# Stick-breaking attention from suffix products and differences of neighbouring values, in place of attention weights

## The chip, the cores and the metric

The kernel runs on one core of one Trainium2 chip. The metric is the device time of one execution in microseconds (us). Before the change three runs gave 1531.31 us as their median (1530.76 to 1535.02).

## The reference, cut to what matters

One layer normalises and modulates a sequence of 2048 rows of 1024 numbers, projects it once to 4232 columns, lets three mixers work on parts of these columns (a gated MLP, an mLSTM, a causal attention of the stick-breaking kind), and projects the gated results back. The change is in the third mixer. It has 6 heads of 64; q and k are normalised; a query block has 128 rows.

```python
z = einsum('bthd,bshd->bhts', q_block, k[:, :kv_len]) * scale
strict = s_idx < t_idx
log_not = where(strict, log_sigmoid(-z), 0)
suffix = cumsum(log_not, reverse=True) - log_not          # over the keys behind s
a = where(strict, exp(log_sigmoid(z) + suffix), 0)
out = einsum('bhts,bshd->bthd', a, v)
```

So a weight is `a_s = sigmoid(z_s)` times the product of `sigmoid(-z)` over the later keys. With `S_s`, the product of `sigmoid(-z)` from key s to the end of the row (1 for masked keys), this is `a_s = S_(s+1) - S_s`. Summed by parts, `sum a_s v_s` is the last value of the row's key range plus `sum S_s (v_(s-1) - v_s)`, with `v_(-1) = 0`.

## The kernel before, in words

The 2048 rows are 16 tiles of 128, in three blocks of 5, 5 and 6 tiles. For each block the modulated rows stay in SBUF, transposed and split in a high and a low part (`hT`); every product with them is three matmuls. The six attention heads are three pairs, p = 0, 1, 2. For every block and pair:

1. `c_proj` projects the pair's q, k and v, one tile at a time: 24 matmuls into one of three PSUM buffers (`pc`). Behind each tile `c_evac` empties the buffer: ScalarE squares q and k (`sq`, L318), VectorE and GpSimd make the scale (`rr`), ScalarE copies v as high part into `Vst` (L323), VectorE writes the low part (L324), and VectorE scales q and k (`qk`, L327). Its second half, one tile later, transposes q and k and writes `Kst` and `Qst`. In the first two blocks the finished pieces go to DRAM for the next block (`k_d`, `v_d`, SyncE's queue).
2. `stick` runs the attention in units: query tile i, head h, up to four key tiles, from the last keys to the first. `front` makes the scores (`z`), two sigmoids on ScalarE (`bb` of -z, L372, and `be` of z, L373), the mask on GpSimd (L375, L377), the suffix product on VectorE (`tensor_tensor_scan`, L380) and the product of both (`be`, L384, units in turn on VectorE and GpSimd). `middle` transposes `be` on TensorE (L395) and splits it in a high and a low part (`aT`: ScalarE L397, VectorE L398). `back` multiplies with `Vst` (L410) and adds the parts (`avs`, `avt`). `fin` sums both halves (`py`), copies (`yc`, L428) and stores. A generator runs front, middle, back and fin one unit apart.

While a pair's units run, the other mixers' projections are woven between them as fillers: `interleave` spreads them by estimated TensorE time. A scheduler then orders the instructions of each engine, by priority and by its own model of time; that order is fixed in the program, and every engine and SyncE's DMA queue works through its list strictly in turn: an instruction that waits holds up all that stand behind it on its engine.

Of the kernel before, what the change touches and what calls it, by code (L numbers as in the profile page):

```python
# [8 lines left out]
F32 = mybir.dt.float32  # L9
F32R = mybir.dt.float32r  # L10
BF16 = mybir.dt.bfloat16
AF = mybir.ActivationFunctionType
ALU = mybir.AluOpType
AX = mybir.AxisListType
PSUM = bass.MemoryType.PSUM
DRAM = bass.MemoryType.DRAM

P = 128
SEQ = 2048
NT = SEQ // P  # L20
# [6 lines left out]
T5 = 6  # L27
OFF = dict(au=0, av=256, az=512, bq=768, bk=1152, bv=1536, bo=1920, bz=2304, bi=2688,
# [4 lines left out]
def hybrid_block_kernel(ctx: ExitStack, tc: tile.TileContext, x, c, norm_g, w_ada, b_ada, w_in,  # L33
                        ga_v_norm, ga_ws, ga_bs, mb_conv_w, mb_conv_b, mb_b_i, mb_b_f, mb_h_norm,
                        sc_q_norm, sc_k_norm, w_out, out):
    nc = tc.nc
# [4 lines left out]
    dram = ctx.enter_context(tc.tile_pool(name="scratch", bufs=1, space=DRAM))  # L41

# [10 lines left out]
    v_d = [dram.tile([P, NT, 2, P], F32, name=f"v_d{p}") for p in range(3)]  # L53

# [1 line left out]
    ident = const.tile([P, P], F32, name="ident")  # L56
# [18 lines left out]
    gates = const.tile([P, 2, NT, 4], F32, name="gates")  # L75
# [69 lines left out]
    def mod_x(i, c0, c1, eng=None):  # L145
        """normalised and modulated, in place"""
        xc = x_cols(i, c0, c1)
        nc.vector.scalar_tensor_tensor(xc, xc, xtiles[i][1], hscale[:, c0:c1], ALU.mult, ALU.mult)
        (eng or nc.gpsimd).tensor_tensor(xc, xc, hshift[:, c0:c1], ALU.add)
# [22 lines left out]
    def weights(src, segs, kps=range(KT // 2), staged=None):  # L172
        """hi and lo parts of the given columns, one tile per 128 rows"""
        W = sum(w for _, w in segs)
        tiles = []
        for kp in kps:
            st = staged[kp] if staged else load_w(src, segs, kp)
            for a in range(2):
                wt = wr_p.tile([P, 2, WMAX], F32R, tag="wr", name=f"wr{ntag[0]}_{kp}_{a}")
                nc.scalar.copy(wt[:, 0, :W], st[:, a, :W])  # L180
                (nc.vector if a == 0 else nc.gpsimd).tensor_tensor(  # L181
                    wt[:, 1, :W], st[:, a, :W], wt[:, 0, :W].bitcast(F32), ALU.subtract)
                tiles.append(wt)
        ntag[0] += 1
        return tiles
# [12 lines left out]
    brow = [stk.tile([P, 512], F32, tag="bb", bufs=4, name=f"brow{n}") for n in range(4)]  # L198
    for n in (2, 0, 3, 1):
        nc.gpsimd.memset(brow[n], 0.0)  # L200
    g_bc = [stk.tile([P, 512], F32, tag="be", bufs=3, name=f"g_bc{n}") for n in range(2)]
# [67 lines left out]
    def hT_half(i, j, hh):  # L269
        """half of the rows of tile j of hT, hi and lo parts"""  # L270
        cols = slice(j * P, (j + 1) * P)
        ks = slice(hh * 4, hh * 4 + 4)
        pt = (pat.tile([P, 4, P], F32, tag="at", name=f"pt{i}_{hh}") if i < BLOCKS[0] else
              pproj.tile([P, 512], F32, tag="proj", name=f"pt{i}_{hh}").rearrange("p (k t) -> p k t", k=4))
        for k in range(4):
            kk = hh * 4 + k
            nc.tensor.transpose(pt[:, k, :], x_cols(i, kk * P, (kk + 1) * P), ident)
        nc.scalar.copy(hT[:, 0, ks, cols], pt)
        nc.vector.tensor_tensor(hT[:, 1, ks, cols], pt, hT[:, 0, ks, cols].bitcast(F32), ALU.subtract)  # L279

    def proj_tc(ps, wt, j, W, ks=range(KT)):
        """psum[t, cols] of t tile j of the block"""
        cols = slice(j * P, (j + 1) * P)
        for k in ks:
            nc.tensor.matmul(ps, lhsT=hT[:, 0, k, cols], rhs=wt[k][:, 0, :W], start=k == 0, stop=False)  # L285
            nc.tensor.matmul(ps, lhsT=hT[:, 0, k, cols], rhs=wt[k][:, 1, :W], start=False, stop=False)  # L286
            nc.tensor.matmul(ps, lhsT=hT[:, 1, k, cols], rhs=wt[k][:, 0, :W], start=False, stop=k == KT - 1)  # L287
            yield 3 * W / 2.4

# [22 lines left out]
    def c_evac(b, t0, p, j, ps):  # L312
        i = t0 + j
        if p == 0:
# [8 lines left out]
        nc.scalar.copy(Vst[:, i, :, 0:64], ps[:, 256:384].rearrange("p (h d) -> p h d", h=2))  # L323
        nc.vector.tensor_tensor(Vst[:, i, :, 64:128], ps[:, 256:384].rearrange("p (h d) -> p h d", h=2),  # L324
                                Vst[:, i, :, 0:64].bitcast(F32), ALU.subtract)
# [6 lines left out]
        for a in range(4):  # L332
# [8 lines left out]
                                       ALU.mult, ALU.subtract)  # L341
        if b < len(BLOCKS) - 1:
            nc.sync.dma_start(k_d[p][:, :, i * P:(i + 1) * P], ks.bitcast(F32))
            nc.sync.dma_start(v_d[p][:, i], Vst[:, i].bitcast(F32))

    def stick(p, t0, nb):
# [12 lines left out]
        st_count = []  # L359

        def front(u):
# [7 lines left out]
            bb = stk.tile([P, 513], F32, tag="bb", bufs=4, name=f"bb{nm}")  # L369
            be = stk.tile([P, 512], F32, tag="be", bufs=3, name=f"be{nm}")  # L370
            nc.gpsimd.memset(bb[:, w:w + 1], 1.0)  # L371
            nc.scalar.activation(bb[:, :w], z[:, :w], AF.Sigmoid, scale=-1.0)  # L372
            nc.scalar.activation(be[:, :w], z[:, :w], AF.Sigmoid)  # L373
            if s1 == i + 1:
                nc.gpsimd.affine_select(out=bb[:, w - P:w], in_=bb[:, w - P:w], pattern=[[-1, P]],  # L375
                                        compare_op=ALU.is_gt, fill=1.0, base=0, channel_multiplier=1)
                nc.gpsimd.affine_select(out=be[:, w - P:w], in_=be[:, w - P:w], pattern=[[-1, P]],  # L377
                                        compare_op=ALU.is_gt, fill=0.0, base=0, channel_multiplier=1)
            rev = bb[:, 0:w + 1][:, ::-1]
            nc.vector.tensor_tensor_scan(rev, rev, rev, carry.get((i, h), 1.0), ALU.mult, ALU.bypass)  # L380
            carry[i, h] = bb[:, 0:1]
            eng = nc.gpsimd if len(st_count) % 2 else nc.vector
            st_count.append(0)
            eng.tensor_tensor(be[:, :w], be[:, :w], bb[:, 1:w + 1], ALU.mult)  # L384
            st[u] = [be, None]
            return 2 * w / 2.4

        def middle(u):
            i, j, h, s0, s1 = u
            nm = f"{p}_{i}_{h}_{s0}"  # L390
            be = st[u][0]
            nb_ = s1 - s0
            at = pat.tile([P, 4, P], F32, tag="at", name=f"at{nm}")
            for s in range(nb_):
                nc.tensor.transpose(at[:, s, :], be[:, s * P:(s + 1) * P], ident)  # L395
# [24 lines left out]
        def fin(u):  # L420
# [7 lines left out]
            nc.scalar.copy(yc, py[:, 0:P])  # L428
# [224 lines left out]
    def first_chunk():  # L653
        """chunk 0 of the mLSTM ahead of the output phase: its gated output and the state after it"""
# [227 lines left out]
    def mlstm(i):  # L882
        """numerator and denominator of chunk i, state after it"""
# [32 lines left out]
    def mixed(i):  # L916
        """the gated outputs of the three mixers, [t, c]"""
# [43 lines left out]
    def chunk_ahead(i):  # L961
        """chunk i from its scores to the turned outputs"""
        yield from mlstm(i)
        mixed(i)
        yield
        yield from turned(i)
# [66 lines left out]
```

## Time and profile before

| | |
|---|---|
| median of three runs | 1531.31 us |
| span of the profiled execution | 1527.0 us |
| outside the span, by the median | 4.3 us |
| TensorE busy (matmul) | 1413.2 us, 93% |
| VectorE busy | 1123.3 us, 74% |
| GpSimd busy | 757.2 us, 50% |
| ScalarE busy | 749.6 us, 49% |
| mean granted TensorE clock | 0.978 of full |

The profile gives the profiled execution's time as its span, 1527.0 us. The attention runs from about 75 us to 1266 us; behind it comes the output phase, which the change leaves alone. Busy time of TensorE counts each matmul with the tail in which its results drain, and matmuls overlap there, so stretches with 100% are those in which no gap is longer than such a tail.

### The profile page before, as it was taken

What the parts mean: (1) busy time and instruction counts of PE and PEld (TensorE: products, weight loads), DVE (VectorE), ACT (ScalarE), POOL (GpSimd) and SP (SyncE); (2) the same over time, 40 slices, a digit from 0 to 9 for tenths busy, and PEclk for the clock granted to TensorE, in tenths of its full rate; (3) what the DMA queues carried; (4) which work ended last, traced back from release to release, by engine and by line L of the source; (5) the groups of instructions that cost most, each with busy time, mean ns of one, the idle gap of its engine ahead of it and who ended that gap; (6) DMA issues with size and microseconds to landing.
All of it is one profiled execution on the core that took longest, in us unless ns stands there. A gap on an engine that the chain in (4) does not pass through costs nothing.

```text
span 1527.0 us, 25375 instructions
## 1 busy us (share of the span) xinstructions
PE 1413.2 (93%) x8468; PEld 1307.1 (86%) x8468; DVE 1123.3 (74%) x1866; ACT 749.6 (49%) x1832; POOL 757.2 (50%) x1228
## 2 busy tenths in 40 slices
PE   5899999889889999988898899999998978999998
PEld 3789999889878999977898699989898956888887
DVE  6787555775997677699699986879968797544444
ACT  2365444454655455557366755656545565211210
POOL 4364544664445544666344554645535246534442
PEclk8899999999999999999999999999999999999999
DMA  9433423334435422523322124112230154546551
GB/s 325 130 92 100 121 80 87 95 109 122 133 93 140 136 69 74 141 53 111 103 63 74 41 63 124 46 48 76 78 89 18 62 189 120 196 128 190 149 158 67
DMA packets 170595, 163.89 MB, mean 107 GB/s; under 512 B 23610, under 2 KB 146904, under 8 KB 170464
## 3 DMA queue, kind: packets, MB, share of 16 engines
q1 hardware_dynamic: 170240, 162.24, 36.1%
q8 instruction: 67, 1.10, 0.3%
q14 instruction: 64, 0.52, 0.1%
q0 software_dynamic: 224, 0.02, 0.0%
HBM read 124.58 MB, written 37.64 MB: 106 GB/s over the span
## 4 chain that ended last, share of the span: by engine, by line
PE 53%; DVE 25%; issue 7%; DMA 6%; POOL 5%; ACT 4%; SPq 0%; DVEq 0%; POOLq 0%; ACTq 0%
DVE bb L380 9%; PE po L946 4%; PE po L948 4%; PE po L947 4%; PE av L410 3%; PE pc L287 3%; DMA st<-in_w_in_dram 3%; PE pc L285 3%; PE pc L286 3%; PE at L395 3%; DVE acc L467 2%; DVE aT L398 2%; PE pg L286 2%; DVE be L384 2%; PE pg L285 2%
## 5 line engine op out<-in xcount | busy, mean ns | idle before, releaser
L380 DVE TENSOR_TENSOR_SCAN bb<-bb,bb 128x513 f32<-128x513 f32 x144 | 198.9, 1382 | 18.4 <-ACT bb L372 18.0
L384 POOL TENSOR_TENSOR be<-be,bb 128x512 f32<-128x512 f32 (+3 forms) x120 | 135.3, 1127 | 125.2 <-DVE bb L380 65.5
L181 POOL TENSOR_TENSOR wr<-st,wr 128x384 fp32r<-128x384 f32 (+1 forms) x132 | 158.4, 1204 | 61.8 <-ACT wr L180 60.0
L180 ACT CAST wr<-st 128x384 fp32r<-128x384 f32 (+1 forms) x264 | 127.3, 522 | 113.0 <-DMA st<-in_w_in_dram 103.2
L410 PE MATMUL av<-aT,Vst 128*128 128x256 f32 x816 | 148.1, 298 | 30.4 <-DVE aT L398 20.8
L410 PEld LDWEIGHTS av<-aT,Vst 128*128 128x128 f32 x816 | 120.6, 192 | 47.5 <-DVE aT L398 30.5
L398 DVE TENSOR_TENSOR aT<-at,aT 128x512 fp32r<-128x512 f32 (+3 forms) x240 | 142.0, 596 | 24.0 <-ACT aT L397 23.6
L372 ACT ACTIVATE bb<-z 128x512 f32<-128x512 f32 (+3 forms) x240 | 131.1, 547 | 53.4 <-PE z L368 47.4
L397 ACT CAST aT<-at 128x512 fp32r<-128x512 f32 (+3 forms) x240 | 126.8, 529 | 51.7 <-PE at L395 50.4
L395 PE MATMUL at<-ident,be 128*128 128x128 f32 x816 | 133.3, 278 | 16.6 <-DVE Qst L340 7.3
L285 PE MATMUL pc<-wr,hT 128*128 128x384 f32 (+1 forms) x384 | 136.0, 356 | 7.2 <-DVE hT L279 6.2
L287 PE MATMUL pc<-wr,hT 128*128 128x384 f32 (+1 forms) x384 | 136.8, 356 | 2.6 <-DVE hT L279 2.6
L181 DVE TENSOR_TENSOR wr<-st,wr 128x384 fp32r<-128x384 f32 (+1 forms) x132 | 103.9, 787 | 47.8 <-ACT wr L180 47.5
L286 PE MATMUL pc<-wr,hT 128*128 128x384 f32 (+1 forms) x384 | 134.7, 351 | 0.0
L373 ACT ACTIVATE be<-z 128x512 f32<-128x512 f32 (+3 forms) x240 | 132.6, 552 | 0.0
L395 PEld LDWEIGHTS at<-ident,be 128*128 128x128 f32 x816 | 98.4, 142 | 28.2 <-DVE aT L398 11.1
L380 DVE TENSOR_TENSOR_SCAN bb<-bb 128x129 f32<-128x129 f32 (+3 forms) x96 | 95.7, 997 | 17.4 <-POOL bb L375 14.5
L946 PE MATMUL po<-wo,yT 128*128 128x512 f32 x256 | 104.8, 409 | 0.3 <-ACT yT L935 0.3
L947 PE MATMUL po<-wo,yT 128*128 128x512 f32 x256 | 102.3, 399 | 0.7 <-POOL wo L853 0.7
L948 PE MATMUL po<-wo,yT 128*128 128x512 f32 x256 | 101.4, 399 | 0.0
L371 POOL MEMSET bb<- 128x1 f32 x240 | 23.4, 98 | 150.6 <-DVE bb L380 98.8
L367 PE MATMUL z<-Kst,Qst 128*128 128x512 f32 (+3 forms) x240 | 93.7, 392 | 3.8 <-ACT be L373 3.7
(272 smaller groups left out, 4098.7 us busy)
## 6 DMA issues: line engine op xcount, KB each, us to landing
st<-in_w_in_dram SPq DMA_DIRECT2D x180, 128.0 KB, 2.4
st<-in_w_in_dram SPq DMA_DIRECT2D x48, 384.0 KB, 3.3
st<-in_w_in_dram SPq DMA_DIRECT2D x48, 192.0 KB, 2.6
wad<-in_w_ada_dram SPq DMA_DIRECT2D x8, 1024.0 KB, 7.3
xo<-in_x_dram SPq DMA_DIRECT2D x16, 512.0 KB, 3.6
out_dram<-o SPq DMA_DIRECT2D x31, 256.0 KB, 2.8
xt<-in_x_dram SPq DMA_DIRECT2D x15, 512.0 KB, 4.4
qk<-qkT_d SPq DMA_DIRECT2D x15, 384.0 KB, 7.5
```

The source lines that it names most:

```text
L181: (nc.vector if a == 0 else nc.gpsimd).tensor_tensor(wt[:, 1, :W], st[:, a, :W], wt[:, 0, :W].bitcast(F32), ALU.subtract)
L285: nc.tensor.matmul(ps, lhsT=hT[:, 0, k, cols], rhs=wt[k][:, 0, :W], start=k == 0, stop=False)
L286: nc.tensor.matmul(ps, lhsT=hT[:, 0, k, cols], rhs=wt[k][:, 1, :W], start=False, stop=False)
L287: nc.tensor.matmul(ps, lhsT=hT[:, 1, k, cols], rhs=wt[k][:, 0, :W], start=False, stop=k == KT - 1)
L380: nc.vector.tensor_tensor_scan(rev, rev, rev, carry.get((i, h), 1.0), ALU.mult, ALU.bypass)
L384: eng.tensor_tensor(be[:, :w], be[:, :w], bb[:, 1:w + 1], ALU.mult)
L395: nc.tensor.transpose(at[:, s, :], be[:, s * P:(s + 1) * P], ident)
L398: nc.vector.tensor_tensor(aT[:, :nb_, 1, :], at[:, :nb_, :], aT[:, :nb_, 0, :].bitcast(F32), ALU.subtract)
L410: nc.tensor.matmul(flat(av), lhsT=Vst[:, s0 + s, h, :], rhs=flat(aT[:, s]), start=(s0 + s == i), stop=(s0 + s == 0))
L946: nc.tensor.matmul(po, lhsT=yT[:, 0, k, :], rhs=wo[k][:, 0, cs], start=k == 0, stop=False)
L947: nc.tensor.matmul(po, lhsT=yT[:, 0, k, :], rhs=wo[k][:, 1, cs], start=False, stop=False)
L948: nc.tensor.matmul(po, lhsT=yT[:, 1, k, :], rhs=wo[k][:, 0, cs], start=False, stop=k == KT - 1)
```

## The change

Only the suffix product `bb` is left in a unit: the second sigmoid (L373), its mask (L377), the memset of a 513th column (L371) and the product (L384) are gone, and `bb` itself is transposed. The values in `Vst` become differences of neighbouring rows. For that `c_evac` copies v to SBUF (`vt`, ScalarE); a DMA moves rows 0 to 126 of `vt` to rows 1 to 127 of another tile (`dv`); row 0 comes from a small DRAM table of last rows (`vl_d`), which each tile writes; GpSimd subtracts; ScalarE and GpSimd write the high and low part. At the end of a query tile `yc` adds the last value, which a DMA has spread over 128 rows (`vlast`), on VectorE. `bb` has six buffers where `bb` and `be` had four and three.

```diff
+    vl_d = dram.tile([3 * NT, P], F32, name="vl_d")
...
-        nc.scalar.copy(Vst[:, i, :, 0:64], ps[:, 256:384].rearrange("p (h d) -> p h d", h=2))
-        nc.vector.tensor_tensor(Vst[:, i, :, 64:128], ps[:, 256:384].rearrange("p (h d) -> p h d", h=2),
-                                Vst[:, i, :, 0:64].bitcast(F32), ALU.subtract)
+        vt = tmp.tile([P, P], F32, tag="vt", name=f"vt{p}_{i}")
+        nc.scalar.copy(vt, ps[:, 256:384])
+        nc.sync.dma_start(vl_d[p * NT + i:p * NT + i + 1, :], vt[P - 1:P, :])
+        dv = tmp.tile([P, P], F32, tag="dv", name=f"dv{p}_{i}")
+        nc.sync.dma_start(dv[1:P, :], vt[0:P - 1, :])
+        if i == 0:
+            nc.gpsimd.memset(dv[0:1, :], 0.0)
+        else:
+            nc.sync.dma_start(dv[0:1, :], vl_d[p * NT + i - 1:p * NT + i, :])
...
+        nc.gpsimd.tensor_tensor(dv, dv, vt, ALU.subtract)
+        dv2 = dv.rearrange("p (h d) -> p h d", h=2)
+        nc.scalar.copy(Vst[:, i, :, 0:64], dv2)
+        nc.gpsimd.tensor_tensor(Vst[:, i, :, 64:128], dv2, Vst[:, i, :, 0:64].bitcast(F32), ALU.subtract)
...
-            bb = stk.tile([P, 513], F32, tag="bb", bufs=4, name=f"bb{nm}")
-            be = stk.tile([P, 512], F32, tag="be", bufs=3, name=f"be{nm}")
-            nc.gpsimd.memset(bb[:, w:w + 1], 1.0)
+            bb = stk.tile([P, 512], F32, tag="bb", bufs=BB, name=f"bb{nm}")
             nc.scalar.activation(bb[:, :w], z[:, :w], AF.Sigmoid, scale=-1.0)
-            nc.scalar.activation(be[:, :w], z[:, :w], AF.Sigmoid)
...
-                nc.gpsimd.affine_select(out=be[:, w - P:w], in_=be[:, w - P:w], pattern=[[-1, P]],
-                                        compare_op=ALU.is_gt, fill=0.0, base=0, channel_multiplier=1)
-            rev = bb[:, 0:w + 1][:, ::-1]
+                if h == 0:
+                    vlast[i] = stk.tile([P, P], F32, tag="vlast", name=f"vlast{p}_{i}")
+                    nc.sync.dma_start(vlast[i], vl_d[p * NT + i:p * NT + i + 1, :].broadcast_to([P, P]))
+            rev = bb[:, 0:w][:, ::-1]
             nc.vector.tensor_tensor_scan(rev, rev, rev, carry.get((i, h), 1.0), ALU.mult, ALU.bypass)
             carry[i, h] = bb[:, 0:1]
-            eng = nc.gpsimd if len(st_count) % 2 else nc.vector
-            st_count.append(0)
-            eng.tensor_tensor(be[:, :w], be[:, :w], bb[:, 1:w + 1], ALU.mult)
...
-            nc.scalar.copy(yc, py[:, 0:P])
+            nc.vector.tensor_tensor(yc, py[:, 0:P], vlast.pop(i), ALU.add)
```

The second half of the difference (the GpSimd and ScalarE lines) stands in the part of `c_evac` that runs one tile later, but the scheduler puts it earlier. On ScalarE, in the second block's first pair (tiles 5 to 9), the order before was this; `sq` is the square of a tile's q and k, `pc` its PSUM buffer:

```order
L318 ACTIVATE sq_5_4193<-pc_5_4153 128x256
L323 CAST Vst<-pc_5_4153 128x2x64
L318 ACTIVATE sq_6_4229<-pc_6_4203 128x256
L323 CAST Vst<-pc_6_4203 128x2x64
L336 ACTIVATE Kst<-pq_5_4239,prm 128x2x128
L337 ACTIVATE Qst<-pq_5_4239,prm 128x256
L318 ACTIVATE sq_7_4276<-pc_7_4250 128x256
L323 CAST Vst<-pc_7_4250 128x2x64
```

The same place on ScalarE now:

```order
L320 ACTIVATE sq_5_4155<-pc_5_4115 128x256
L326 COPY vt_5_4161<-pc_5_4115 128x128
L353 CAST Vst<-dv_5_4164 128x2x64
L320 ACTIVATE sq_6_4195<-pc_6_4169 128x256
L326 COPY vt_6_4201<-pc_6_4169 128x128
L344 ACTIVATE Kst<-pq_5_4209,prm 128x2x128
L345 ACTIVATE Qst<-pq_5_4209,prm 128x256
L353 CAST Vst<-dv_6_4204 128x2x64
L320 ACTIVATE sq_7_4249<-pc_7_4223 128x256
L326 COPY vt_7_4255<-pc_7_4223 128x128
```

The write of a tile's differences now stands ahead of the square of the next tile, and it can run only when the shifted rows have arrived and GpSimd has subtracted.

At the end of the same stage ScalarE's list now holds this (`bb` are sigmoids of the first attention units, `wr` weights of the next filler):

```order
L383 ACTIVATE bb_5_0_4_4402<-z_5_0_4_4399 128x256
L353 CAST Vst<-dv_8_4312 128x2x64
L320 ACTIVATE sq_9_4357<-pc_9_4331 128x256
L182 CAST wr_3_0_4436<-st_3_4434 128x384
L182 CAST wr_3_1_4439<-st_3_4434 128x384
L326 COPY vt_9_4363<-pc_9_4331 128x128
L383 ACTIVATE bb_5_0_0_4452<-z_5_0_0_4449 128x512
L344 ACTIVATE Kst<-pq_8_4371,prm 128x2x128
L345 ACTIVATE Qst<-pq_8_4371,prm 128x256
L383 ACTIVATE bb_5_1_4_4473<-z_5_1_4_4470 128x256
L353 CAST Vst<-dv_9_4366 128x2x64
L383 ACTIVATE bb_5_1_0_4523<-z_5_1_0_4520 128x512
```

Weights of the next filler and the first units' sigmoids stand behind the differences of tiles 8 and 9. On SyncE's DMA queue there are four transfers more per tile:

```order
L327 DMA vl_d<-vt_5_4161 1x128
L329 DMA dv_5_4164<-vt_5_4161 127x128
L333 DMA dv_6_4204<-vl_d 1x128
L389 DMA vlast_5_4407<-vl_d 128x128
L357 DMA v_d_71<-Vst 128x256
L327 DMA vl_d<-vt_6_4201 1x128
L329 DMA dv_6_4204<-vt_6_4201 127x128
```

The store of tile 5's differences (`v_d`) stands ahead of the shift of tile 6.

## Rows read from the trace of the kernel before

**Rows 1.** The page's head and its part 1: busy us, share, instructions.

```profile
span 1527.0 us, 25375 instructions
PE 1413.2 (93%) x8468; PEld 1307.1 (86%) x8468; DVE 1123.3 (74%) x1866; ACT 749.6 (49%) x1832; POOL 757.2 (50%) x1228
```

**Rows 2.** Windows where VectorE is fullest: length; busy of each engine; clock; DMA.

```profile
375.00:500.00 125.00, 112.56 (x710) 103.99 (x709) 109.01 (x173) 68.95 (x170) 65.31 (x110) 0.99 0.43 123
650.00:700.00 50.00, 42.96 (x259) 39.55 (x258) 46.47 (x76) 28.38 (x75) 31.45 (x53) 0.97 0.24 66
770.00:900.00 130.00, 117.31 (x701) 108.27 (x701) 120.77 (x184) 87.59 (x188) 60.57 (x112) 0.97 0.20 57
1050.00:1100.00 50.00, 47.30 (x291) 45.06 (x291) 47.44 (x78) 32.40 (x82) 27.16 (x49) 0.97 0.20 51
1225.00:1266.00 41.00, 30.64 (x193) 24.42 (x192) 37.46 (x47) 24.37 (x52) 14.82 (x28) 0.96 0.41 148
sum 396.00, PE 350.78 PEld 321.30 DVE 361.15 ACT 241.69 POOL 199.31; mean PE 70.16 PEld 64.26 DVE 72.23 ACT 48.34 POOL 39.86
```

**Rows 3.** The same five windows, line L384 (the removed product) alone: their sum.

```profile
sum 396.00, DVE 33.66 POOL 63.11; mean DVE 6.73 POOL 12.62
```

**Rows 4.** Four other windows (75-300, 500-650, 900-1050, 1100-1150), all instructions: their sum.

```profile
sum 575.00, PE 563.79 PEld 547.41 DVE 408.27 ACT 310.48 POOL 295.26; mean PE 140.95 PEld 136.85 DVE 102.07 ACT 77.62 POOL 73.82
```

**Rows 5.** Waits of TensorE: line, waited for; total us, times, longest us.

```profile
PE av L410 <- DVE aT L398: 20.8, 22, 2.6
PE av L410 <- DVE avt L416: 9.5, 11, 1.8
PE at L395 <- DVE aT L398: 7.1, 12, 1.2
```

**Rows 6.** Groups: line, engine, operation, shapes, count; busy us, mean ns; idle before.

```profile
L384 POOL TENSOR_TENSOR be<-be,bb 128x512 f32<-128x512 f32 (+3 forms) x120 | 135.3, 1127 | 125.2 <-DVE bb L380 65.5
L384 DVE TENSOR_TENSOR be<-be,bb 128x512 f32<-128x512 f32 (+3 forms) x120 | 81.3, 677 | 1.9 <-POOL be L377 0.2
L373 ACT ACTIVATE be<-z 128x512 f32<-128x512 f32 (+3 forms) x240 | 132.6, 552 | 0.0
L377 POOL TENSOR_SCALAR_AFFINE_SELECT be<-be 128x128 f32<-128x128 f32 x96 | 40.6, 423 | 20.6 <-ACT be L373 18.1 <-DMA gate_d<-gg 1.1 <-PE pb L455 0.5
L324 DVE TENSOR_TENSOR Vst<-pc,Vst 128x128 fp32r<-128x128 f32 x48 | 13.3, 281 | 2.1 <-ACT Vst L323 2.1
L416 DVE TENSOR_TENSOR avt<-av,avs 128x128 f32<-128x128 f32 x96 | 26.6, 277 | 25.3 <-ACT avs L414 25.1
L533 POOL TENSOR_TENSOR gu<-tb 128x128 f32<-128x128 f32 x32 | 19.8, 618 | 24.4 <-DVE tb L532 23.3 <-PE pa L287 0.8
```

**Rows 7.** Line L380, VectorE: count, duration ns smallest/median/largest.

```profile
L380 DVE TENSOR_TENSOR_SCAN bb<-bb,bb x144: 1268/1278/3400, 114.7 to 1257.9; 128x513 f32<-128x513 f32 x144
```

**Rows 8.** ScalarE in time, 504 to 510 us: start, us, instruction [idle before <-releaser].

```profile
504.77 0.39 ACT L318 ACTIVATE sq<-pc 128x256 f32<-128x256 f32 x1 [2.54 <-PE pc L287]
505.05 0.26 ACT L323 CAST Vst<-pc 128x128 fp32r<-128x128 f32 x1
...
509.42 0.39 ACT L318 ACTIVATE sq<-pc 128x256 f32<-128x256 f32 x1 [1.10 <-PE pc L287]
```

**Rows 9.** Transfers yc to y_d: issue ns on SyncE; KB and us to landing.

```profile
L429 SPq DMA_DIRECT2D y_d<-yc x48: 319/339/1277, 112.3 to 1266.1; - x48
y_d<-yc SPq DMA_DIRECT2D x48, 64.0 KB, 1.7
```

**Rows 10.** DMA, 509.5 to 511 us: one store of k, 256 pieces of 512 bytes.

```profile
DMA packets 272, 0.13 MB, mean 87 GB/s; under 512 B 16, under 2 KB 272, under 8 KB 272
q1 hardware_dynamic: 272, 0.13, 30.8%
```

**Rows 11.** DMA, 1.7 to 2.2 us: one load of 8 rows of 512 bytes.

```profile
DMA packets 16, 0.00 MB, mean 8 GB/s; under 512 B 8, under 2 KB 16, under 8 KB 16
```

More of the change, by code (lines that the diff above doesn't have):

```diff
@@ L27 @@
 T5 = 6
+BB = 6
 OFF = dict(au=0, av=256, az=512, bq=768, bk=1152, bv=1536, bo=1920, bz=2304, bi=2688,
@@ L197, in hybrid_block_kernel @@
     crow = tmp.tile([8, P], F32, tag="t512", bufs=T5, name="crow")
-    brow = [stk.tile([P, 512], F32, tag="bb", bufs=4, name=f"brow{n}") for n in range(4)]
+    brow = [stk.tile([P, 512], F32, tag="bb", bufs=BB, name=f"brow{n}") for n in range(4)]
     for n in (2, 0, 3, 1):
         nc.gpsimd.memset(brow[n], 0.0)
-    g_bc = [stk.tile([P, 512], F32, tag="be", bufs=3, name=f"g_bc{n}") for n in range(2)]
+    g_bc = [stk.tile([P, 512], F32, tag="bb", bufs=BB, name=f"g_bc{n}") for n in range(2)]
     def ada_load(half):
@@ L358, in stick @@
         st = {}
-        st_count = []
+        vlast = {}
         def front(u):
@@ L376, in front @@
                                         compare_op=ALU.is_gt, fill=1.0, base=0, channel_multiplier=1)
-                nc.gpsimd.affine_select(out=be[:, w - P:w], in_=be[:, w - P:w], pattern=[[-1, P]],
-                                        compare_op=ALU.is_gt, fill=0.0, base=0, channel_multiplier=1)
-            rev = bb[:, 0:w + 1][:, ::-1]
+                if h == 0:
+                    vlast[i] = stk.tile([P, P], F32, tag="vlast", name=f"vlast{p}_{i}")
+                    nc.sync.dma_start(vlast[i], vl_d[p * NT + i:p * NT + i + 1, :].broadcast_to([P, P]))
+            rev = bb[:, 0:w][:, ::-1]
             nc.vector.tensor_tensor_scan(rev, rev, rev, carry.get((i, h), 1.0), ALU.mult, ALU.bypass)
             carry[i, h] = bb[:, 0:1]
-            eng = nc.gpsimd if len(st_count) % 2 else nc.vector
-            st_count.append(0)
-            eng.tensor_tensor(be[:, :w], be[:, :w], bb[:, 1:w + 1], ALU.mult)
-            st[u] = [be, None]
+            st[u] = [bb, None]
             return 2 * w / 2.4
@@ L390, in middle @@
             nm = f"{p}_{i}_{h}_{s0}"
-            be = st[u][0]
+            bb = st[u][0]
             nb_ = s1 - s0
@@ L394, in middle @@
             for s in range(nb_):
-                nc.tensor.transpose(at[:, s, :], be[:, s * P:(s + 1) * P], ident)
+                nc.tensor.transpose(at[:, s, :], bb[:, s * P:(s + 1) * P], ident)
             aT = stk.tile([P, 4, 2, P], F32R, tag="aT", bufs=3, name=f"aT{nm}")
```

## The prediction

> **What bounds the kernel now.** I read the busy shares first, then windows by stage, then who TensorE waits for, and last the stretch in which v is written. TensorE is the fullest engine, 93% of a span of 1527.0 us [rows 1], and the change gives it neither more nor fewer matmuls. So the change can only move TensorE's idle time. Its place shows in the windows: in five stretches of the attention, together 396 us, VectorE is busy 361.15 us (91%) and TensorE 350.78, so idle 45.2 us [rows 2]; in four others, 575 us, VectorE is busy 408.27 (71%) and TensorE idle only 11.2 us [rows 4]. TensorE is late where VectorE is full. The waits agree: the three largest of its attention lines end with VectorE, on the split of the transposed weights and on the sum of the two output parts, 20.8 + 9.5 + 7.1 = 37.4 us [rows 5]. [...]
>
> The reader is also to see the start of each attention stage. While a pair's q, k and v are projected, ScalarE waits for TensorE, does the square (0.39 us) and the copy of v (0.26 us), and waits again; one tile follows the other after 509.42 - 504.77 = 4.65 us [rows 8]. Nothing is full there, but everything passes through ScalarE in turn.
>
> **The change part by part.** *What goes.* ScalarE loses the second sigmoid, 240 of 552 ns, 132.6 us [rows 6]. It is not the bound (49%, [rows 1]), so I count nothing for it beyond a shorter way from score to scan. GpSimd loses its share of the product, 135.3 us, and the second mask, 40.6 us [rows 6]; it is not the bound either. VectorE loses 120 products of 677 ns, 81.3 us [rows 6], of which 33.66 us lie in the five full stretches [rows 3]. There it is the late engine, so this part counts: 33.7 us. The rest, 47.6 us, lies mostly where TensorE has hardly any idle time to give back; I count 4 us.
>
> *What eases.* The scan takes 1278 ns in the median and 3400 at the longest for the same shape [rows 7]; GpSimd reads the same memory at those times, and its work falls by 135.3 + 40.6 us and grows by the 59 us below. I take 6 us in the full stretches, between nothing and a sixth of the 45.2 us. So the gain is 33.7 + 4 + 6 = 44 us. Its bounds: nothing, if the fixed order of the instructions keeps TensorE waiting as it does; and 45.2 + 10 = 55 us, all idle time of the five stretches with the clock that it costs.
>
> *What stays even.* VectorE loses the low part of v, 48 of 281 ns [rows 6], and gets the sum into yc, the same number of the same shape from PSUM, nearest to the 277 ns of avt [rows 6]: nothing either way. ScalarE writes v twice instead of once and yc no more: even. `vlast` is asked for as a query tile begins and needed at its end, some units later; I count nothing, and where it came late VectorE's whole list would stand behind it.
>
> *What is added, and waits.* GpSimd gets two 128x128 subtractions per tile, 96 of 618 ns by the nearest row [rows 6], 59 us on a half-empty engine: nothing by itself. But they and ScalarE's write stand in a chain. From the copy of v: SyncE issues the row store and the shift (2 x 0.34 us [rows 9]), the shift lands, GpSimd subtracts (0.62), ScalarE writes the high part (0.26), and only behind it, in ScalarE's list as the change orders it, come the next tile's square (0.39) and copy (0.26). That is 2.21 us plus the landing. If the sum is under the 4.65 us between tiles, the wait costs nothing; if it is over, each tile puts ScalarE further behind, and with it the weights of the next filler, the first sigmoids and the emptying of PSUM buffers, all queued behind the write.
>
> The landing has two bounds. Low: 1.7 us, the median of a transfer of the same 64 KB in the same 512-byte pieces [rows 9]; the chain is 3.9 us, hidden. High: the pieces go one after another. One store of 256 such pieces kept 30.8% of 16 engines busy for 1.5 us, 7.4 us for 272 packets, 27 ns each [rows 10]. The 64 KB of [rows 9] are 128 pieces, 8 for each of 16 engines; 127 on one engine are 119 more in a row, 3.2 us more: landing 4.9 us, chain 7.1 us, 2.5 us too long per tile. Which is nearer? The store of 128 rows closes with 16 small packets [rows 10], the load of 8 rows with 8 [rows 11]: the number of engines follows the rows, with equal shares. 127 is prime, so equal shares leave one engine. I take the high bound, 4.9 us.
>
> [...]
>
> What does it cost? A stage has five or six tiles, so four or five follow-ups of 2.5 us, 10 to 12.5 us by which ScalarE would be late at the end where the chain is whole (the second block's first pair). In other stages the scheduler set two copies ahead of one write, or the tiles come slower, and part of it goes. TensorE can run on for as long as the three `pc` buffers and the two score buffers last, about one to two tiles, 4.65 to 9.3 us. So the loss of a stage lies between nothing and 8 us; I take 4 us, the middle, for nine stages: 36 us.
>
> The sum: 1527.0 - 44 + 36 = 1519 us of span; with the 4.3 us by which the median of the runs stands over this span, 1523 us.
>
> **The rivals.** *A. The shift is hidden.* It lands in about the 1.7 us of its like, or TensorE's lead covers the chain. For it: nothing in the trace waits long for a 64 KB transfer between tiles, and ScalarE has idle time of 1.1 to 2.5 us before each square [rows 8]. Against it: 127 rows have no equal shares. It gives the whole gain: 1527 - 44 + 4 = 1487 us, at best 1527 - 55 + 4 = 1476.
>
> *B. The shift becomes the bound of every stage start: slower.* One mechanism: the rows pass one DMA engine, ScalarE stands at the write of the differences, and TensorE uses up its buffers and stops. It decides once the chain passes 4.65 us by more than the buffers cover, that is, over some 2 us per tile. At 8 us for each of nine stages the loss is 72 us: 1527 - 44 + 72 + 4 = 1559 us; with half of the gain lost too, 1581. For it: the list of ScalarE, and the one engine. Against it: in six of nine stages the writes are grouped behind later squares.
>
> *C. The relief doesn't come.* The full stretches are bound by the order in which the units interleave, not by VectorE's load. Then only a small loss or nothing: 1527 to 1540 us. For it: the idle times are short (the longest wait is 2.6 us [rows 5]). Against it: their release by VectorE nearly everywhere.
>
> **How the numbers follow.** Forecast (both effects, near 1523, with 1505 to 1540 as its own range) 0.42; A 0.26; B 0.27; C 0.05. The range reaches into A and B, from 1478 to 1570 us, and leaves out about 0.08 below and 0.10 above. A measurement of this kernel can tell 0.3%, 4.6 us, from no change. Faster by more: all of A, and over half of the forecast's own case (0.23), 0.49. Within: a quarter of that case and part of C, 0.13. Slower by more: B, a fifth of the forecast's case, and part of C, 0.38.
>
> **What would show it.** In the five stretches VectorE's share should fall from 91% to about 82% and TensorE's waits for aT and avt from 37.4 us to under 20. The shift's transfers should land 4.9 us after issue; a landing near 2 us makes A right. ScalarE should wait at the write of `Vst`, and GpSimd at its subtraction, for the DMA, some microseconds per tile; the squares of successive tiles should lie 7 us apart instead of 4.65 where the chain is whole. TensorE's new idle time should lie in the ten microseconds behind each projection of q, k and v. I am wrong in the size if that idle time is under 15 us or over 60 us in total, and in the mechanism if VectorE's relief leaves its waits as they were.

## The result, and the profile after

The changed kernel takes 1569.27 us (median of four runs, 1566.2 to 1571.08), the kernel before 1533.16 us (four runs beside it, 1530.76 to 1535.09). The ratio is 1.0238, with a 95% interval of 1.0216 to 1.026: slower by 36 us, where 1523 us and a gain were forecast. Rival B came, at 1569 instead of its 1559 us. The head of the page after answers to [rows 1]:

```profile
span 1564.5 us, 24609 instructions
PE 1427.1 (91%) x8468; PEld 1316.1 (84%) x8468; DVE 1015.6 (65%) x1746; ACT 645.5 (41%) x1592; POOL 606.4 (39%) x871
```

Three engines lost 104 to 151 us of work each, and TensorE's count of matmuls is the same. Of the 37.5 us by which the span is longer, 23.6 are new idle time of TensorE (113.8 us before, 137.4 now), and 13.9 are matmuls that took longer. The stages have moved, so the windows of [rows 2] no longer hold the same work. Two stretches do, from the last square of one stage to the first of the next, behind the second block's and the third block's first pair. The first two lines are of the kernel before, the others of the changed one (length; busy us of TensorE, its weight loads, VectorE, ScalarE, GpSimd; clock; DMA):

```profile
384.23:501.53 117.30, 104.86 (x663) 96.42 (x663) 102.58 (x161) 64.42 (x160) 61.28 (x104) 0.99 0.45 126
770.05:924.22 154.17, 141.48 (x857) 131.49 (x856) 138.96 (x211) 102.15 (x219) 74.88 (x132) 0.98 0.21 60
412.05:524.04 111.99, 103.49 (x646) 94.89 (x647) 91.19 (x153) 55.07 (x135) 41.94 (x63) 0.98 0.46 130
818.12:962.90 144.78, 138.56 (x849) 130.60 (x849) 123.81 (x198) 83.70 (x178) 45.09 (x65) 0.98 0.26 76
```

VectorE is down from 87 to 81% in the first and from 90 to 86% in the other, and TensorE's idle time in them from 12.4 to 8.5 us and from 12.7 to 6.2. The relief shows there, so the new idle time lies elsewhere. TensorE's waits in the whole kernel, those of [rows 5] first (total us, times, longest):

```profile
PE av L418 <- DVE aT L406: 10.4, 11, 4.0
PE av L418 <- DVE avt L424: 8.4, 12, 1.2
PE at L403 <- DVE aT L406: 2.1, 4, 0.9
...
PE z L380 <- ACT bb L383: 15.4, 7, 3.2
PE pq L341 <- DVE qk L335: 15.0, 9, 2.9
```

The 37.4 us on aT and avt are 20.9: the relief came. In their place stand waits for ScalarE's sigmoids of the attention units and for the scaled q and k of the projection. The waits of the three engines behind the shift:

```profile
ACT Vst L353 <- POOL dv L351: 193.5, 45, 7.5
POOL dv L351 <- DMA dv<-vt: 117.0, 39, 5.2
DVE qk L335 <- POOL rr L324: 44.4, 32, 4.5
```

ScalarE stands 193.5 us at the write of the differences, in 45 of 48 tiles. ScalarE in time, in the stage of the second block's first pair (compare [rows 8]):

```profile
388.63 0.30 ACT L353 CAST Vst<-dv 128x128 fp32r<-128x128 f32 x1 [6.22 <-POOL dv L351]
388.83 0.38 ACT L320 ACTIVATE sq<-pc 128x256 f32<-128x256 f32 x1
389.11 0.26 ACT L326 COPY vt<-pc 128x128 f32<-128x128 f32 x1
389.25 0.49 ACT L344 ACTIVATE Kst<-pq,prm 128x256 fp32r<-128x256 f32 x1
389.62 0.48 ACT L345 ACTIVATE Qst<-pq,prm 128x256 fp32r<-128x256 f32 x1
396.20 0.30 ACT L353 CAST Vst<-dv 128x128 fp32r<-128x128 f32 x1 [6.09 <-POOL dv L351]
396.40 0.38 ACT L320 ACTIVATE sq<-pc 128x256 f32<-128x256 f32 x1
```

The square no longer waits for TensorE but follows the write at once, 396.40 - 388.83 = 7.57 us after the one before; 4.65 us it was. The chain between, on SyncE's queue and GpSimd:

```profile
389.50 0.34 SPq L357 DMA_DIRECT2D v_d<-Vst  x1
389.93 0.24 SPq L327 DMA_DIRECT2D vl_d<-vt  x1
390.22 0.66 SPq L329 DMA_DIRECT2D dv<-vt  x1
```

```profile
388.13 0.46 POOL L351 TENSOR_TENSOR dv<-dv,vt 128x128 f32<-128x128 f32 x1 [3.73 <-DMA dv<-vt]
389.00 0.46 POOL L354 TENSOR_TENSOR Vst<-dv,Vst 128x128 fp32r<-128x128 f32 x1 [0.41 <-ACT Vst L353]
389.76 0.19 POOL L323 TENSOR_SCALAR rr<-rr 128x4 f32<-128x4 f32 x1 [0.29 <-DVE rr L322]
390.03 1.01 POOL L324 TENSOR_TENSOR rr<-rr,neghalf 128x4 f32<-128x4 f32 x1
395.70 0.46 POOL L351 TENSOR_TENSOR dv<-dv,vt 128x128 f32<-128x128 f32 x1 [4.66 <-DMA dv<-vt]
```

From the shift's issue at 390.22 to the subtraction at 395.70 pass 5.48 us; over the 48 tiles the median is 5.80 (worked out from the start times of the two lines). A stretch of 1.8 us with almost nothing but one shift in it, that of a later tile, shows why (GB/s in 40 equal slices; packets; share of 16 engines):

```profile
GB/s 0 0 0 23 23 0 0 23 23 23 23 23 23 23 23 23 23 11 23 23 23 23 23 23 23 23 23 23 23 11 23 23 23 23 23 23 23 23 23 11
DMA packets 74, 0.03 MB, mean 19 GB/s; under 512 B 7, under 2 KB 74, under 8 KB 74
q1 hardware_dynamic: 74, 0.03, 6.7%
```

From the eighth slice on there are two packets in a slice of 45 ns at most, a steady 23 GB/s; over the stretch 6.7% of 16 engines are busy, which is 1.07 engines. Ahead of it, packets of this shift begin 1.3 us after its issue (802.24 us), another transfer of 192 KB passes between them, and the row of them ends at 807.3: 5.1 us, where 4.9 were predicted. GpSimd's subtraction comes only at 808.26.

### The profile page after: what moved, and what is told of

Its sections match the earlier page's. It is cut to its first block, busy times and chain, and to the rows that moved or that the text cites. A ratio compares the mean times of both kernels' runs of the same rounds, so it can differ in the third digit from the quotient of the medians.

```text
span 1564.5 us, 24609 instructions
## 1 busy us (share of the span) xinstructions
PE 1427.1 (91%) x8468; PEld 1316.1 (84%) x8468; DVE 1015.6 (65%) x1746; ACT 645.5 (41%) x1592; POOL 606.4 (39%) x871
## 5 line engine op out<-in xcount | busy, mean ns | idle before, releaser
L391 DVE TENSOR_TENSOR_SCAN bb<-bb,bb 128x512 f32<-128x512 f32 x144 | 193.0, 1341 | 9.4 <-ACT bb L383 8.5
L183 POOL TENSOR_TENSOR wr<-st,wr 128x384 fp32r<-128x384 f32 (+1 forms) x132 | 154.6, 1175 | 104.9 <-ACT wr L182 97.5
L403 PE MATMUL at<-ident,bb 128*128 128x128 f32 x816 | 133.2, 276 | 17.1 <-DVE Qst L348 10.6
L403 PEld LDWEIGHTS at<-ident,bb 128*128 128x128 f32 x816 | 98.6, 141 | 27.5 <-issue 10.2
L380 PE MATMUL z<-Kst,Qst 128*128 128x512 f32 (+3 forms) x240 | 95.1, 399 | 19.5 <-ACT bb L383 15.4
L461 PE MATMUL pb<-hT,wr 128*128 128x320 f32 (+1 forms) x288 | 95.7, 333 | 10.1 <-ACT wr L182 4.3
L385 POOL TENSOR_SCALAR_AFFINE_SELECT bb<-bb 128x128 f32<-128x128 f32 x96 | 43.5, 455 | 152.9 <-ACT bb L383 131.6
L391 DVE TENSOR_TENSOR_SCAN bb<-bb 128x128 f32<-128x128 f32 (+3 forms) x96 | 83.6, 874 | 26.0 <-POOL bb L385 25.7
L463 PE MATMUL pb<-hT,wr 128*128 128x320 f32 (+1 forms) x288 | 94.5, 330 | 3.6 <-POOL wr L183 2.8
```

Of the source, the lines that this page charges most:

```text
L183: (nc.vector if a == 0 else nc.gpsimd).tensor_tensor(wt[:, 1, :W], st[:, a, :W], wt[:, 0, :W].bitcast(F32), ALU.subtract)
L403: nc.tensor.transpose(at[:, s, :], bb[:, s * P:(s + 1) * P], ident)
```

## The experiments

Theory 1: the 127 rows pass one DMA engine, and what stands behind their landing in the lists of ScalarE and GpSimd holds TensorE up. The main rival: the loss is that of more transfers, of another order, or of a relief that doesn't come. "Stretch" below is the time from the first to the last square (L320), summed over the nine stages, and "to subtraction" the median from the shift's issue to GpSimd's subtraction; both are worked out from start times in the trace. Ratios are to the kernel before, on the same chip.

| kernel | us | ratio, 95% interval | to subtraction, us | stretch, us |
|---|---|---|---|---|
| before | 1530 to 1533 | 1 | | 197.2 |
| after | 1569.27 | 1.0238 (1.0216 to 1.026) | 5.80 | 241.1 |
| relief alone | 1480.24 | 0.965 (0.9634 to 0.9667) | | 189.5 |
| chain alone | 1612.63 | 1.052 (1.0505 to 1.0536) | 5.35 | 248.2 |
| cut 113 + 14 | 1550.05 | 1.0111 (1.0086 to 1.0135) | 5.53 | 225.9 |
| cut 122 + 5 | 1504.88 | 0.9831 (0.981 to 0.9853) | 4.02 | 196.7 |
| cut 126 + 1 | 1499.46 | 0.9778 (0.9764 to 0.9793) | 3.61 | 191.1 |
| cut 112 + 15, first | 1489.80 | 0.9736 (0.9696 to 0.9775) | 3.31 | 190.1 |
| high part by GpSimd | 1543.44 | 1.0073 (1.0044 to 1.0102) | 5.83 | 208.1 |
| tied to the next tile | 1520.90 | 0.9933 (0.991 to 0.9956) | 7.35 | 188.5 |
| tied, cut 112 + 15 | 1486.74 | 0.971 (0.9686 to 0.9735) | 7.56 | 191.9 |

**The shift in two, 126 + 1 and 113 + 14.** The two cuts have the same number of transfers, one more than the change; the second has 113 and 14 in place of the two numbers of rows.

```diff
-        nc.sync.dma_start(dv[1:P, :], vt[0:P - 1, :])
+        nc.sync.dma_start(dv[1:P - 1, :], vt[0:P - 2, :])
+        nc.sync.dma_start(dv[P - 1:P, :], vt[P - 2:P - 1, :])
```

> The shift of 127 rows is issued as two transfers, one of 126 rows and one of the last row; the data is the same. Theory 1 (the 127 rows pass one DMA engine; the write of the differences stands in ScalarE's list behind them at every stage start): 126 has the divisor 14, so nine rows on each of 14 engines; from the issue to GpSimd's subtraction 2 to 3.5 us instead of 5.8, squares of neighbouring tiles 4.6 to 5.5 us apart instead of 7.6, ScalarE's wait at the write of Vst from 193.5 us to under 60, and the time 1485 to 1505 us. Theory 2 (the loss is that of the two more transfers per tile in SyncE's queue and of a third engine in the chain, whatever the shift takes): there is one transfer more, so 1565 to 1580 us.

> The same edit with another cut: 113 rows and 14 rows, the same number of transfers as in the cut of 126 and 1. 113 is prime. Theory 1: 113 rows still pass one engine, 14 x 27 ns = 0.4 us less than 127: issue to subtraction 5.0 to 6 us, squares over 7 us apart, the time 1550 to 1575 us. Theory 2: as the cut of 126 and 1, within 0.5%. A third reading, that two transfers are simply better than one: both clearly faster than 1569.

Theory 1 held in both, the second at the lower end of its range. With 126 + 1 rows the kernel is 70 us faster than the changed one and faster than the kernel before; with 113 + 14 it stays slower than before. More transfers are not the harm, and two are not the cure. DMA at a shift of 126 rows, 0.7 us:

```profile
DMA packets 146, 0.08 MB, mean 111 GB/s; under 512 B 26, under 2 KB 145, under 8 KB 145
q1 hardware_dynamic: 145, 0.06, 34.4%
```

Its 126 packets pass in that time; the shift of 127 rows above took 3.8 us for them, with the other transfer between. The wait at the write falls with it, from 193.5 us, though not under the 60 expected, and the way to the subtraction is 3.61 us, not 2 to 3.5:

```profile
ACT Vst L354 <- POOL dv L352: 74.8, 33, 5.8
```

**The relief alone, the chain alone.** The first keeps the new attention and writes `Vst` from PSUM as before, the low part by VectorE; it leaves out the shift and the differences, but keeps the copy and the row store. The second keeps the old attention and feeds `Vst` by the shift. The edit of the first, in its main lines:

```diff
# relief alone, in c_evac
-        nc.sync.dma_start(dv[1:P, :], vt[0:P - 1, :])
...
+        nc.scalar.copy(Vst[:, i, :, 0:64], ps[:, 256:384].rearrange("p (h d) -> p h d", h=2))
...
-        nc.gpsimd.tensor_tensor(dv, dv, vt, ALU.subtract)
...
-        nc.scalar.copy(Vst[:, i, :, 0:64], dv2)
```

> The relief alone: the attention of the changed kernel (one sigmoid, one mask, no product, vlast added at the end), but Vst is written from PSUM as in the kernel before. Left out are the shift and the differences, so the weights multiply v itself and the output is another. Theory 1: the relief that the prediction counted comes, 1483 to 1497 us (1533 less 36 to 50). Rival (the relief does not come, the full stretches are bound by the order of the units): 1525 to 1538, and the chain would cost only some 35 us.

> The chain alone: the attention of the kernel before with its second sigmoid, masks and product, and Vst fed by the copy, the shift, GpSimd's subtraction and ScalarE's write as in the changed kernel (for room vt takes a slot of the 2 KB tiles). Left out is what makes the differences fit, so the output is another. Theory 1: before plus 70 to 85 us, 1603 to 1618. Rival (the chain costs only 35 us and the relief nothing): 1560 to 1575.

The relief is 1532.53 - 1480.24 = 52 us, just over theory 1's range, and its rival is out. The chain costs 80 us on the kernel before and 1569.27 - 1480.24 = 89 us on the relief. TensorE's waits in the relief alone:

```profile
PE av L412 <- DVE avt L418: 8.2, 12, 1.2
PE av L412 <- DVE aT L400: 7.1, 10, 1.9
```

**Whose list stands.** The high part goes to GpSimd, so ScalarE has nothing behind the shift any more.

```diff
-        nc.scalar.copy(Vst[:, i, :, 0:64], dv2)
+        nc.gpsimd.tensor_copy(Vst[:, i, :, 0:64], dv2)
```

> The shift of 127 rows on one engine stays; only the high part of the differences is written by GpSimd, so that nothing in ScalarE's list stands behind the shift. GpSimd's list still does: behind the subtraction of a tile come there the two operations on rr of the next tile, which VectorE needs for its q and k. Theory 1a (ScalarE's list carries the loss): 1485 to 1505 us, squares 5 us apart. Theory 1b (GpSimd's list carries it as well): the tiles keep their distance of 7 us or more, 1550 to 1580 us, and VectorE waits for rr at qk.

26 us better than the changed kernel, 63 worse than the relief alone: between the two, and 1b missed the distance of the tiles, which grew little (the stretch is 208.1 us). The wait has moved to VectorE:

```profile
DVE qk L335 <- POOL rr L324: 102.1, 42, 5.9
```

44.4 us it was in the changed kernel, and 22.4 in the relief alone. GpSimd's list holds the next tile's `rr` behind the subtraction, and VectorE needs it. Both lists carry the loss.

**Another place in the list.** The shift stays on one engine; a false dependence puts the subtraction behind the next tile's square, copy and `rr`.

```diff
+        zc = tmp.tile([P, 1], F32, tag="zc", bufs=3, name=f"zc{p}_{i}")
+        nc.gpsimd.tensor_scalar(zc, rr[:, 0:1], 0.0, None, ALU.mult)
+        zlast[0] = zc
...
+        nc.gpsimd.tensor_tensor(vt[:, 0:1], vt[:, 0:1], zlast[0], ALU.add)
         nc.gpsimd.tensor_tensor(dv, dv, vt, ALU.subtract)
```

> The shift of 127 rows on one engine stays, but each subtraction is tied to the next tile: 0 times rr of the next tile is added to a column of vt, so that the subtraction, and ScalarE's write behind it, stand behind the square, the copy and rr of the next tile (two more 128x1 operations on GpSimd per tile). Theory 1 (the loss is that the lists stand behind the landing, not that the shift is slow): the shift has the distance of two tiles, 2 x 4.9 us against a chain of 7.5, so it is hidden; from issue to subtraction 6 to 8 us, yet squares about 5 us apart and the time 1483 to 1503 us. Rival (the one engine is slow for all transfers that share it, or SyncE's queue is the brake): 1550 to 1575 us.

The lengthening of the stretch is gone (188.5 us, 189.5 in the relief) and 48 us of time with it, though the 127 rows still go in one transfer: the larger part of the cost is the place in the list. But 1520.9 lies between the two readings' ranges; 41 us over the relief are left, and with a fast shift beside the tie 34 of them go too (below). ScalarE in that kernel, at the end of a stage:

```profile
405.30 0.30 ACT L359 CAST Vst<-dv 128x128 fp32r<-128x128 f32 x1 [3.47 <-POOL dv L357]
405.50 0.59 ACT L389 ACTIVATE bb<-z 128x512 f32<-128x512 f32 x1
...
409.47 0.30 ACT L359 CAST Vst<-dv 128x128 fp32r<-128x128 f32 x1 [2.54 <-POOL dv L357]
409.68 0.47 ACT L349 ACTIVATE Kst<-pq,prm 128x256 fp32r<-128x256 f32 x1
```

Sigmoids, and even q and k of the last tile, stand behind writes that wait.

**How many engines.** The cut of 122 + 5 rows (the diff is that of 126 + 1 with other numbers), and both mends together, with 112 + 15 rows issued ahead of the row store and the tie.

> The shift in two transfers of 122 and 5 rows. If the number of engines is the largest divisor up to 16, 122 = 2 x 61 has two engines of 61 rows each; between the cuts of 126 (9 rows per engine, 1499 us) and 113 (113 rows, 1550). On a line through these two, 0.49 us per row: 1525 us, 1515 to 1535, issue to subtraction about 4.5 us. If only a prime number of rows is slow (any even number is spread over many engines): 1495 to 1505.

> [...] Theory 1: nothing stands behind the shift any more; what is left over the relief alone (1480 us) is GpSimd's work and SyncE's issues: 1480 to 1495 us. If a rest of the chain stays whatever the landing: 1497 to 1510.

The time fell into the range of the other reading, 1495 to 1505, but the trace shows that 122 rows pass two engines and not many. DMA in 1.85 us of one:

```profile
DMA packets 137, 0.07 MB, mean 40 GB/s; under 512 B 8, under 2 KB 136, under 8 KB 136
q1 hardware_dynamic: 136, 0.07, 13.2%
```

13.2% of 16 are 2.1 engines, and the rate is 44 GB/s in most slices of this stretch, against the 23 of one. Taken as 113 rows on one engine and 61 on each of two, the way to the subtraction is 5.53 - 4.02 = 1.51 us shorter by 52 rows, 29 ns per row; the one engine of the 113 rows is not shown by itself. But the time is not on the line between the other cuts: 1504.88, not 1525. With 5.80, 5.53, 4.02, 3.61 and 3.31 us to the subtraction the kernels take 1569, 1550, 1505, 1499 and 1490 us: the first 1.8 us bring 64 us, the next 0.7 us 15. With 122 rows the squares already lie 5.29 us apart in the median, against 7.45 in the changed kernel and 4.84 in the relief alone (start times in the traces). Both mends give 1486.74 us, the fastest kernel of the study that leaves nothing out, 2.9% under the kernel before and 6.5 us over the relief alone.

**Without the tie, and by DRAM.** The cut of 112 + 15 alone; the rows stored to DRAM and loaded one row higher (128 rows each way), without and with the tie; and the kernel before without VectorE's products, for the parts of the relief. The first differs from the cut of 126 + 1 in its numbers and in that the store of the last row stands behind the shift; the main edits of the others are these:

```diff
-        nc.sync.dma_start(vl_d[p * NT + i:p * NT + i + 1, :], vt[P - 1:P, :])
+        nc.sync.dma_start(vs_d[p][1 + i * P:1 + (i + 1) * P, :], vt)
...
-        nc.sync.dma_start(dv[1:P, :], vt[0:P - 1, :])
+        nc.sync.dma_start(dv, vs_d[p][i * P:(i + 1) * P, :])
```

```diff
-            eng = nc.gpsimd if len(st_count) % 2 else nc.vector
             st_count.append(0)
-            eng.tensor_tensor(be[:, :w], be[:, :w], bb[:, 1:w + 1], ALU.mult)
+            if len(st_count) % 2 == 0:
+                nc.gpsimd.tensor_tensor(be[:, :w], be[:, :w], bb[:, 1:w + 1], ALU.mult)
```

> The shift in two transfers of 112 and 15 rows, issued ahead of the row store, and nothing else (the subtraction is not tied to the next tile). If a fast landing alone does it: 1485 to 1495 us, as with the tie (1487). If a rest of the chain stays that only the tie removes: 1496 to 1503, as the cut of 126 and 1 (1499).

> No transfer of 127 rows: the 128 rows of v are stored to DRAM and loaded again one row higher, 128 rows each way, and the last row comes from the same table; two transfers per tile in place of three. Each is spread like the other transfers of 128 rows, but the load must wait for the store. Theory 1 (the time between the copy and the subtraction decides, whatever it consists of): two landings of 1.7 to 2.2 us and two issues, 4.5 to 6 us, so 1510 to 1560 us. Rival (only the one engine is harmful): 1485 to 1500.

> The same way through DRAM with the subtraction tied to the next tile. Theory 1: as the 127 rows with the tie (1521) or better, 1490 to 1520 us; a rest is left where the first two tiles of a stage come close together and at its last tile. Rival (only the one engine is harmful): 1480 to 1490.

> The kernel before without the 120 products on VectorE (left out, so that half of the units go on with the second sigmoid unmultiplied); the second sigmoid, both masks, GpSimd's products and the write of Vst from PSUM stay. If the relief is VectorE's: 1485 to 1495 us, 38 to 48 of the 52 us that the relief alone brought. If a good part of it comes from ScalarE's and GpSimd's lighter lists (the shorter way from score to scan): 1500 to 1515 us.

The cut alone gives 1489.80 (0.9736, 0.9696 to 0.9775), not to be told from the tied one. The way through DRAM gives 1501.40 (0.981, 0.978 to 0.984): twice the bytes, a round trip, 4.61 us from the store's issue to the subtraction, and 68 us faster than 127 rows within SBUF. My 1510 was too high, as on the cut of 122. With the tie it is 1504.71 (0.9834, 0.9783 to 0.9884), no better. Without VectorE's products the kernel before takes 1495.68 (0.9773, 0.9743 to 0.9804), at the edge of the first reading: 35 of the 52 us go with VectorE's products, and 17 with the rest of the change. The lighter lists of ScalarE and GpSimd are the likely cause of these, but no run takes the rest apart.

**The last tile of a stage.** Fast shift there alone, with the tie; slow there alone; fast there alone without the tie.

```diff
+        if j == BLOCKS[b] - 1:
+            nc.sync.dma_start(dv[1:113, :], vt[0:112, :])
+            nc.sync.dma_start(dv[113:P, :], vt[112:P - 1, :])
+        else:
+            nc.sync.dma_start(dv[1:P, :], vt[0:P - 1, :])
```

> The subtraction is tied to the next tile as before (1521 us with the shift on one engine in every tile), and only in the last tile of each stage, nine of 48, the shift goes in 112 and 15 rows. Theory 1 (what the tie leaves belongs to the last tile, which has no next one): most of the 34 us to the kernel with both mends goes with nine tiles, 1487 to 1500 us. Rival (the rest is spread over the tiles or belongs to the slow transfers as such): nine tiles of 48, 1512 to 1520.

> No tie; the shift goes in 112 and 15 rows in all tiles but the last of each stage, where the 127 rows stay on one engine. Theory 1: the stretch of the squares is gone and the loss behind the last tile stays: 1490 plus 25 to 40, 1515 to 1530 us. Rival (the loss is spread evenly): 1490 plus nine of 48 parts of 79, 1500 to 1508.

> The reverse: no tie, the 127 rows stay on one engine in all tiles but the last of each stage, where the shift goes in 112 and 15 rows. Theory 1: the stretch stays and the loss behind the last tile goes: 1569 less 25 to 40, 1529 to 1544 us. Rival (spread evenly): 1569 less nine of 48 parts of 79, 1550 to 1558.

They gave 1505.64 (0.9839, 0.9804 to 0.9874), 1500.45 (0.9801, 0.9781 to 0.9821) and 1562.28 (1.0205, 1.0186 to 1.0224). The first and the third lie outside both of their ranges, the second in that of the rival. My theory of the last tile falls. Without the tie nine slow tiles cost 11 us over the cut of 112 + 15, where the shift also stands ahead of the row store, and 1 us over the cut of 126 + 1 (1499.46), where it stands behind it as here. Nine fast tiles bring 7 us, 5 by the ratios, whose intervals touch. All of this is under their share of nine in 48, 15 of 79 us. With the tie they bring 15 of 34 us, more than their share; that the last tile alone has no next one to hide behind fits this, but is not shown.

## Why the prediction was wrong

**The relief** was right and a little small: 44 us predicted, between 0 and 55; 52 measured. VectorE's products were taken at 33.7 + 4 us; leaving them out gave 35. The rest, counted as 6 us from scans that ease, was 17. The scans are only a part of that: the 144 with a carry took 1382 ns in the mean before and 1341 after, 6 us in the whole kernel, where 6 had been counted for the full stretches alone. In the kernel before, the 75 of them during which GpSimd did nothing took 1276 ns in the mean and 1290 at the most, the other 69 took 1496 (worked out from start times and durations). No run shows the 10 us that the upper bound holds for the clock of the five stretches; over the whole span the granted clock was 0.983 in the relief alone and 0.973 in the kernel before beside it (medians of the runs), by estimate 16 us of full-clock time. The waits for aT and avt fell from 37.4 to 20.9 us, not under 20.

**The landing** was right in its mechanism and nearly so in its size. 127 rows on one engine, 4.9 us predicted; in the one shift read the packets end 5.1 us after the issue. That the two agree so well is in part luck: the packets follow each other every 24 ns, 3.0 us for 127, and the rest is the start of 1.3 us and the other transfer between them. What the chain waits for comes later still: from issue to subtraction pass 5.28 us at the least and 5.80 in the median. That the number of engines follows the rows with equal shares was inferred from [rows 10] and [rows 11]; the stretches read agree, with 6.7% of 16 engines (1.07) for 127 rows and 13.2% (2.1) for 122. At the 126 rows 34.4% were busy over 0.7 us, 5.5 engines in the mean with what else passed, so the 14 of the expectation are not shown as such. For 113 only the median to the subtraction speaks, 5.53 us against 3.61 with 126 + 1. For 112 + 15 it is 3.31; how many engines these rows pass is not shown.

**The chain** was right: 7.1 us predicted, 7.57 us between squares where it is whole. The difference lies in SyncE's queue, on which the store of the previous tile's differences stands ahead and was not counted: the copy of v ends at 389.37 us, that store is issued at 389.50, once GpSimd has written the low part at 389.46, and the row store only at 389.93. These 0.56 us, and 5.48 us from the shift's issue to the subtraction where 0.34 + 4.9 were counted, are in part made up by shorter steps on GpSimd and ScalarE (the subtraction takes 0.46 us, not 0.62).

**The step that failed** is the loss of a stage: "between nothing and 8 us; I take 4 us, the middle, for nine stages: 36 us". The chain cost 89 us, 9.9 per stage, over the upper end. Of the relief alone the page has this:

```profile
PE 1402.9 (95%) x8468; PEld 1305.8 (88%) x8468; DVE 1023.4 (69%) x1794; ACT 647.0 (44%) x1592; POOL 560.5 (38%) x772
```

Its span is 1479.8 us, that of the changed kernel 1564.5. Of the 84.7 us between these two profiled executions, 60.5 are idle time of TensorE (76.9 and 137.4 us), 6.7 per stage, and 24.2 are the same 8468 matmuls taking longer, 2.7 per stage. Four things in that step were wrong:

- *TensorE's buffers were taken as cover.* The prediction had ScalarE 10 to 12.5 us late in a whole stage and set the buffers against it, 4.65 to 9.3 us. The traces show far less cover. Here are the nine stretches, summed, in the relief alone and in the changed kernel, and then the 10 us behind each of them, likewise:

```profile
sum 189.52, PE 188.18 PEld 184.35 DVE 105.07 ACT 77.53 POOL 66.05; mean PE 20.91 PEld 20.48 DVE 11.67 ACT 8.61 POOL 7.34
sum 241.12, PE 207.96 PEld 196.85 DVE 89.13 ACT 72.09 POOL 84.34; mean PE 23.11 PEld 21.87 DVE 9.90 ACT 8.01 POOL 9.37
sum 90.00, PE 89.50 PEld 87.32 DVE 71.97 ACT 62.08 POOL 54.01; mean PE 9.94 PEld 9.70 DVE 8.00 ACT 6.90 POOL 6.00
sum 90.00, PE 66.59 PEld 60.86 DVE 52.68 ACT 42.21 POOL 52.60; mean PE 7.40 PEld 6.76 DVE 5.85 ACT 4.69 POOL 5.84
```

  The stretches are 51.6 us longer, and TensorE stands idle in them for 33.2 us instead of 1.3: it ran on for some 20 us at the most, 2 per stage. Behind them it stands idle for another 23.4 us, 0.5 in the relief. The prediction looked for all of its new idle time there, and for 60 us at the most. Without any cover its own figures for six stages of five tiles and three of six would have given 6 x 10 + 3 x 12.5 = 97.5 us, nearer to the 89, though these come in part by the other ways named here.
- *The clock was put at nothing.* It was counted only as a bound of the gain. The first of these windows of 10 us reads, in the changed kernel:

```profile
87.95:97.95 10.00, 6.18 (x31) 6.04 (x32) 4.95 (x10) 3.61 (x13) 4.96 (x13) 0.66 0.42 122
```

  The granted clock is 0.66 to 1.00 in the nine of them, and 1.00 in all nine in the relief alone. From 409 to 417 us it is 0.50 in the changed kernel; a matmul of 128x320 (`pb`) took 0.47 us there, and 0.31 from 417.6 us on. In the trace one starts 0.27 and 0.15 us after the other at these clocks, so their records overlap. Over the whole span the mean is 0.968 against 0.979, some 19 us of full-clock time, of the order of the 24.2 us.
- *The grouping was counted as protection.* "In six of nine stages the writes are grouped behind later squares". Against the relief alone, the stretch rose by 4.3 to 11.9 us in eight of nine stages, and by 0.9 in one.
- *One list was looked at.* The prediction put the wait into ScalarE's list. With ScalarE free 63 us were still lost: GpSimd's `rr` stands behind the subtraction too, and VectorE waits for it; this list was not read. SyncE's queue is a third one. Its store of the differences waits for GpSimd with the next shift behind it:

```profile
SPq L357 <- POOL Vst L354: 50.1, 18, 4.6
```

Slow last tiles make 1 to 11 us of the 89. How the 89 us divide among the three lists stays open, as do the last 19 us that the tied kernel with fast last tiles (1505.64) lacks to the one with all tiles fast (1486.74).

**Of the rivals**, B was right in its mechanism, with 72 us for the loss. Its condition, "over some 2 us per tile", fits: the whole chain is 2.9 us over, and with 4.02 us to the subtraction, 1.8 us less, 25 us of the 89 are left, with 5.53 us 70. A's price of 1487 us is what the kernel gives once the shift is hidden (1486.74), but so closely only by luck: the relief is 8 us more than counted, and a rest of 6.5 us stays. C is out.

## What to carry to other kernels

A wait that recurs with every tile is priced first as its excess over the distance of the tiles, times the number of tiles. Buffers come off that sum only where a trace shows them to cover: here they covered 2 us per stage where 4.65 to 9.3 were set, idle time went on behind the last tile, and a lower clock came on top. Read the list of every engine that stands in the chain, and of the DMA queue, behind the waiting instruction, not only the one where the wait stands. Before a gain is given up for a slow transfer, change its row count: here 126 + 1 rows in place of 127 made a kernel 2.4% slower into one 2.2% faster.

## What the runs showed of the hardware

- The transfer of 127 rows of 512 bytes within SBUF ran at 23 GB/s on one engine where nothing passed between, a packet every 24 ns (6.7% of 16 engines busy), and the round trip of 128 rows through DRAM had its data back sooner (4.61 against 5.80 us from issue to subtraction).
- The issue of a transfer on SyncE differs with its number of rows, but not in proportion to it. Medians of 48 within SBUF: 555 ns for 112 rows, 656 for 127, 658 for 113, 681 for 122, 739 for 5, 846 for 126, 851 for 14, 857 for 15. The load of 128 rows from DRAM took 320.
